# Sparse attention in a two-layer decoder: transposes of the projections held behind parts of the blocks that follow them, and other homes for the keys' rows and the compressions' sums

## The chip, the cores and the metric

The kernel runs on one core of a Trainium2 chip (trn2). A core has five engines that run side by side, each through its own queue, in order: TensorE (PE, matrix products and transposes, which write into PSUM), VectorE (DVE), ScalarE (ACT), GpSimd (POOL) and SyncE (SP, which here only issues the loads of weights from the chip's memory). The metric is the time of one execution in microseconds on the device, over several runs; lower is better.

## The reference

The input is 256 tokens of 1024 numbers. Two layers follow, each a token mixer and a squared-ReLU MLP with norms around them. The first mixer is native sparse attention, and the edit lies in it:

```python
proj = h @ w_in                       # q (16 heads x 64), then kc, vc, ks, vs, kw, vw (4 groups x 64 each), gate
q, kc_t, ks, kw = rope(q), rope(kc_t), rope(ks), rope(kw)
kcmp = silu(windows(kc_t + pos) @ w1[0]) @ w2[0]      # 15 windows of 32 tokens, 16 apart
vcmp = silu(windows(vc_t + pos) @ w1[1]) @ w2[1]
o = g0 * attend(q, kcmp, vcmp) + g1 * attend(q, selected ks, vs) + g2 * attend(q, kw, vw)
m = o @ w_out
```

With 256 tokens all four blocks of 64 are selected, so the second branch sees all causal keys. The second layer's mixer (FoX) and both MLPs are not touched.

## The kernel before, in words

Every large product is done in three: a weight and an activation are split in a high and a low part (fp32r), and `mm3` (lines 152 to 156) adds hi × hi, hi × lo and lo × hi. A weight chunk of 512 KB comes through `load_w` (line 116): SP loads it into a `raw` tile (three of them), ACT casts `hi` out of it, DVE subtracts to get `lo` (`split`, lines 112 to 114); there are six hi and six lo tiles.

The sparse mixer is a list of blocks. `c0` and `c1` are the projections kc and vc, which the compression reads; `k0`, `k1` the keys ks and kw; `v0` is vs, `v1` is vw with the gates; `q0` to `q3` are four heads of q each. Each block is 48 products on the two halves of the tokens (`nsa_block`), with two chunks of weights (v1 has three); they add up in a PSUM bank called ps_m, of which there are two. A block's evacuation (`c_evac`, `k_evac`, `q_evac`) applies rope on DVE (three operations that read the bank, and an add), and makes from it rows in SBUF (kd, kk, qs). The second step of an evacuation transposes these rows on PE into one of two ps_t banks, and ACT copies them out (tokT, kT, qT). `p0` and `p1` are the compressions (`compress`): first DVE adds positions into win (which needs tokT) and splits it, then 32 products with four chunks, whose sums ACT and DVE bring out as hs and hid; the last step transposes hid, applies silu and multiplies with w2.

The order is written in PLAN (line 45). There a name starts a block, `>p0` takes a compression one step further, `+k0` finishes an evacuation, that is, issues its transposes. S, C, V and T with numbers are the parts of the attention that follow. But this order is not the one on the engines: the framework's scheduler takes instructions as their inputs come and gives each engine a fixed list; only instructions passed to `keep_in_program_order` stand on their engine where the program has them. Before, the scheduler put a transpose among the products where it thought fit.

Of the kernel before, what the change touches and what calls it, by code (L numbers as in the profile page):

```python
# [9 lines left out]
R = mybir.dt.float32r  # L10
# [3 lines left out]
P = 128  # L14
# [6 lines left out]
G = 4  # L21
# [20 lines left out]

PLAN = "c0 +c0 v0 p0 c1 +c1 k0 k1 >p0 +k0 v1 +k1 +p0 p1 q0 >p1 +p1 | q1 q2 +q0 +q1 S02 C00 S00 S01 V00 q3 +q2 V01 S03 V02 +q3 C01 T00 S05 V03 S04 V04 S06 V05 C10 S12 S07 V06 S10 T02 S11 T01 V10 V12 V07 S15 V11 S13 C11 V13 / T03 S14 S16 T10 V16 S17 V17 V14 V15 T13 T11 T12"
SB_B = 4
FB = 2
VG = 3
# [18 lines left out]
def kernel(ctx, tc, x_in, norm_g, w_up, w_down, nsa_w_in, nsa_pos, nsa_w1, nsa_w2,  # L67
# [14 lines left out]
    def ps_tile(use):  # L82
        return psum.tile([P, 512], F32, name="ps_" + use)
# [248 lines left out]
    def c_evac(j, pv):  # L332
        kd = ev.tile([P, NT, G, 2, DH], F32, name="kd", tag="b4")
        if j == 0:
            rope(kd[:, :, :, 0, :], pv, rot)
            act.copy(kd[:, :, :, 1, :], kd[:, :, :, 0, :])
        else:
            for t in range(NT):
                v_copy(kd[:, t], pv[:, t].unsqueeze(2).broadcast_to([P, G, 2, DH]), t)
        yield  # L340
        for t in range(NT):
            pt = ps_tile("t")
            for g in range(G):
                pe.transpose(pt[:, g * P:(g + 1) * P], kd[:, t, g].rearrange("p u d -> p (u d)"), ident)
            ptv = pt.rearrange("p (g t) -> p g t", g=G)
            act.copy(tokT[j][0:DH, :, t * P:(t + 1) * P], ptv[0:DH])
            act.copy(tokT[j][DH:P, :, max(0, t * P - 1):(t + 1) * P - 1], ptv[DH:P, :, 1 - t:P])

    def k_evac(br, pk):
        kr = ev.tile([P, NT, G, DH], F32, name="kr")  # L350
        rope(kr, pk, rot)
        kks = []
        for t in range(NT):
            kk = ev.tile([P, G, 4, DH], R, name="kk", tag="b4")
            krb = kr[:, t].unsqueeze(2).broadcast_to([P, G, 2, DH])
            act.copy(kk[:, :, 0:2, :], krb)
            dve.tensor_tensor(out=kk[:, :, 2:4, :], in0=krb, in1=kk[:, :, 0:2, :].bitcast(F32), op=OP.subtract)
            kks.append(kk)
        yield
# [18 lines left out]
    def q_evac(c, pv):  # L378
# [4 lines left out]
        yield  # L383
        for t in range(NT):
            qT[t, c] = nsa1.tile([P, G, P], R, name="qT", bufs=6)
            pt = ps_tile("t")
            for j in range(G):
                pe.transpose(pt.bitcast(R)[:, j * P:(j + 1) * P], qs[:, t, j, :], ident_r)
            act.copy(qT[t, c], pt.rearrange("p (h t) -> p h t", h=G))

    def nsa_block(c0, ws=None, between=None):

        ws = ws or load_cols(W, c0, BW)
        ps = ps_tile("m").rearrange("p (t n) -> p t n", t=NT)
        hk = KD // 2 if between is None else KD
        for k0 in range(0, KD, hk):
            for t in range(NT):
                if between:

                    for i, (a, b) in enumerate(((0, 0), (0, 1), (1, 0))):  # L400
                        for k in range(KD // 2):
                            pe.matmul(ps[:, t, :], tok(hT, k, t)[a], ws[k][b], start=i + k == 0, stop=False)
                    between()
                for k in range(KD // 2 if between else k0, k0 + hk):
                    mm3(ps[:, t, :], tok(hT, k, t), ws[k], t == 0 and k == 0, t == NT - 1 and k == KD - 1)
                between = None
# [11 lines left out]
    def compress(j):  # L418
# [20 lines left out]
        hs = cp.tile([NW, CH], F32, name="hs")  # L439
        act.copy(hs, ps[64:64 + NW, 0:CH])  # L440
# [1 line left out]
        yield  # L442
        pt = ps_tile("t")
        for k in range(2):
            pe.transpose(pt[:, k * 64:k * 64 + NW], hid[:, k * P:(k + 1) * P], ident[0:NW, 0:NW])
# [6 lines left out]
        if j == 0:  # L452
            hidT = cp.tile([P, 2, P], F32, name="hidTk")
            pool.memset(hidT, 0.0)
            dve.tensor_tensor(out=hidT[:, :, 0:NW], in0=ptv, in1=sg, op=OP.mult)
            for k in range(2):
                pe.matmul(po[:, 0:P], w2[:, j, k].rearrange("p u d -> p (u d)"), hidT[:, k, :], start=(k == 0), stop=(k == 1))
            pk = po[:, 0:NW].rearrange("p (g c) -> p g c", g=G)
            split(kc[:, :, 0, 0:NC_], kc[:, :, 1, 0:NC_], pk)
        else:  # L460
            hidT = cp.tile([P, 2, G, REP, 32], F32, name="hidTv", tag="win")
            pool.memset(hidT, 0.0)
            for k in range(2):
                a, b = (v[:, k, :].rearrange("p (g c) -> p g c", g=G).unsqueeze(2).broadcast_to([P, G, REP, NC_])
                        for v in (ptv, sg))
                dve.tensor_tensor(out=hidT[:, k, :, :, 0:NC_], in0=a, in1=b, op=OP.mult)
            for g in range(G):
                for k in range(2):
                    pe.matmul(po[:, g * DH:(g + 1) * DH], hidT[:, k, g].rearrange("p r c -> p (r c)"),
                              w2[:, j, k, 0, :], start=(k == 0), stop=(k == 1))  # L470
            pv = po[:, 0:G * DH].rearrange("p (g d) -> p g d", g=G)
            for r in range(REP):
                rows = slice(r * 32, (r + 1) * 32)
                (act.copy if r % 2 else dve.tensor_copy)(vc[rows, :, r, 0:DH], pv[rows])

# [57 lines left out]
    def pair_s(t, p):  # L533
# [59 lines left out]
    env, scores, oc, on = {}, {}, {}, {}  # L593
    for cmd in PLAN.split():
        op, arg = cmd[0], cmd[1:]
        if op == "+":
            finish(env.pop(arg))
        elif op == ">":
            next(env[arg])
        elif cmd in gens:  # L600
            env[cmd] = gens[cmd]()
            if op != "v":
                next(env[cmd])
        elif op == "|":
            cmp_ctx.close()
            at = nsa_ctx.enter_context(tc.tile_pool(name="at", bufs=2))
# [441 lines left out]
```

## Time and profile before

| | |
|---|---|
| median of 3 runs | 670.02 us (667.80 to 670.09) |
| the profiled execution | 668.77 us, of which 667.0 is the span from the first to the last instruction |
| busy share of the span | PE 97%, its weight loads 85%, DVE 67%, ACT 56% |
| mean granted clock of TensorE | 0.996 of full |
| loads | 110.17 MB, 165 GB/s on the mean |

One execution was profiled, and all rows are from it, in microseconds from its first instruction. A row of a timeline gives start, length, engine, line, operation and, in brackets, how long the engine had been idle and which operation ended that. Products are pipelined, so one's length (0.28) is more than the distance to the next (0.12).

### The profile page before, as it was taken

Reading aid. Unit: us, or ns where it says so; the run is one execution under the profiler, and the core shown is the slowest. Engines: PE = TensorE matmul, PEld = TensorE weight load, DVE = VectorE, ACT = ScalarE, POOL = GpSimd, SP = SyncE. Lnnn points to the kernel's source line nnn. Section 1 sums busy time; section 2 is a strip of 40 time slices with the busy share of each in tenths; the row PEclk is TensorE's granted clock in tenths of the full one; section 3 lists DMA queues with packets and bytes.
Section 4 is the critical chain, followed back from the end, with each engine's and each line's share of the span. In section 5 each row is a group of like instructions: output and inputs, shape, how many; then the busy total and the mean of one; then the engine's idle time right before and its main releaser. Section 6 shows DMA issues by size and latency. Waiting matters only on the chain.

```text
span 667.0 us, 10515 instructions
## 1 busy us (share of the span) xinstructions
PE 649.2 (97%) x3953; PEld 564.1 (85%) x3953; DVE 445.3 (67%) x854; ACT 375.2 (56%) x654; POOL 37.6 (6%) x77
## 2 busy tenths in 40 slices
PE   7999999999999999999999999999999999999996
PEld 6999998888788888888889999987878888888884
DVE  5787898764985756556649677873967566566533
ACT  5768487765774645445537566663675445454411
POOL 1000003212100000000005000000100000000000
PEclk9998999999999999999999999999999999999999
DMA  9676853201696746656554863541667476565301
GB/s 306 179 200 192 241 168 97 64 1 60 196 305 198 230 153 217 193 164 215 166 151 115 270 216 96 158 125 35 193 185 231 149 220 190 165 213 180 104 1 63
DMA packets 74802, 110.17 MB, mean 165 GB/s; under 512 B 4696, under 2 KB 60672, under 8 KB 74752
## 3 DMA queue, kind: packets, MB, share of 16 engines
q1 hardware_dynamic: 72336, 105.48, 51.3%
q10 hardware_dynamic: 2416, 4.03, 2.0%
q8 instruction: 31, 0.51, 0.3%
q14 instruction: 19, 0.16, 0.1%
HBM read 108.44 MB, written 1.05 MB: 164 GB/s over the span
## 4 chain that ended last, share of the span: by engine, by line
PE 85%; DVE 5%; DMA 5%; ACT 2%; issue 2%; POOL 1%; SPq 0%; POOLq 0%; DVEq 0%; ACTq 0%
PE ps_m L735 14%; PE ps_m L736 8%; PE ps_m L154 6%; PE ps_m L156 6%; PE ps_m L155 6%; PE ps_o L155 5%; PE ps_s L156 5%; PE ps_s L154 5%; PE ps_o L154 5%; PE ps_s L155 5%; PE ps_o L156 5%; PE ps_o L571 3%; DVE lo L114 2%; PE ps_m L738 2%; PE ps_t L566 2%
## 5 line engine op out<-in xcount | busy, mean ns | idle before, releaser
L114 DVE TENSOR_TENSOR lo<-raw,hi 128x1024 fp32r<-128x1024 f32 (+2 forms) x196 | 237.0, 1213 | 117.4 <-ACT hi L113 110.5
L113 ACT CAST hi<-raw 128x1024 fp32r<-128x1024 f32 (+2 forms) x196 | 203.4, 1043 | 130.9 <-DMA raw<-in_mlp_w_up_dram 42.1
L735 PE MATMUL ps_m<-hT,hi 128*128 128x512 f32 x392 | 140.1, 396 | 0.0
L736 PE MATMUL ps_m<-hT,lo 128*128 128x256 f32 x448 | 116.3, 280 | 0.0
L736 PEld LDWEIGHTS ps_m<-hT,lo 128*128 128x128 f32 x448 | 84.5, 189 | 5.0
L735 PEld LDWEIGHTS ps_m<-hT,hi 128*128 128x128 f32 x392 | 73.6, 188 | 16.2
L154 PE MATMUL ps_m<-hi,hT 128*128 128x256 f32 (+3 forms) x236 | 76.3, 324 | 0.8 <-ACT hT L113 0.8
L155 PE MATMUL ps_m<-hi,hT 128*128 128x256 f32 (+3 forms) x236 | 75.6, 320 | 1.4 <-DVE hT L114 1.3
L156 PE MATMUL ps_m<-lo,hT 128*128 128x256 f32 (+3 forms) x236 | 75.2, 318 | 0.9 <-DVE lo L114 0.9
L155 PE MATMUL ps_o<-hi,ul 128*128 128x512 f32 x128 | 50.6, 396 | 0.0
L156 PE MATMUL ps_s<-lo,uh 128*128 128x512 f32 x128 | 50.6, 395 | 0.0
L154 PE MATMUL ps_o<-hi,uh 128*128 128x512 f32 x128 | 50.5, 395 | 0.0
L154 PE MATMUL ps_s<-hi,uh 128*128 128x512 f32 x128 | 50.5, 395 | 0.0
L155 PE MATMUL ps_s<-hi,ul 128*128 128x512 f32 x128 | 50.5, 394 | 0.0
L156 PE MATMUL ps_o<-lo,uh 128*128 128x512 f32 x128 | 50.4, 394 | 0.0
L154 PEld LDWEIGHTS ps_m<-hi,hT 128*128 128x128 f32 x236 | 45.2, 192 | 4.6 <-ACT hT L113 1.3
L155 PEld LDWEIGHTS ps_m<-hi,hT 128*128 128x128 f32 x236 | 45.3, 192 | 4.4 <-DVE hT L114 2.4
L156 PEld LDWEIGHTS ps_m<-lo,hT 128*128 128x128 f32 x236 | 45.1, 191 | 3.7 <-DVE lo L114 1.3
L740 ACT COPY second<-ps_m 128x256 f32<-128x256 f32 x56 | 20.8, 371 | 38.6 <-PE ps_m L738 38.6
L154 PE MATMUL ps_m<-hT,hi 128*128 128x256 f32 x128 | 37.5, 293 | 0.0
L155 PE MATMUL ps_m<-hT,lo 128*128 128x256 f32 x128 | 36.2, 283 | 0.0
L156 PE MATMUL ps_m<-hT,hi 128*128 128x256 f32 x128 | 36.1, 282 | 0.0
(242 smaller groups left out, 1107.4 us busy)
## 6 DMA issues: line engine op xcount, KB each, us to landing
raw<-in_mlp_w_up_dram SPq DMA_DIRECT2D x64, 512.0 KB, 4.1
raw<-in_mlp_w_down_dram SPq DMA_DIRECT2D x64, 512.0 KB, 4.3
raw<-in_fox_w_in_dram SPq DMA_DIRECT2D x22, 512.0 KB, 4.2
raw<-in_nsa_w_in_dram SPq DMA_DIRECT2D x18, 512.0 KB, 4.9
raw<-in_nsa_cmp_w_dram SPq DMA_DIRECT2D x8, 512.0 KB, 4.5
raw<-in_nsa_w_out_dram SPq DMA_DIRECT2D x8, 512.0 KB, 3.6
raw<-in_fox_w_out_dram SPq DMA_DIRECT2D x8, 512.0 KB, 4.3
gb<-in_norm_g_dram ACTq DMA_DIRECT2D x7, 512.0 KB, 6.6
```

Source lines behind the costliest of these rows:

```text
L113: act.copy(hi, src)
L114: dve.tensor_tensor(out=lo, in0=src, in1=hi.bitcast(F32), op=OP.subtract)
L154: queue(pe.matmul(ps, lhs[0], rhs[0], start=start, stop=False))
L155: queue(pe.matmul(ps, lhs[1], rhs[0], start=False, stop=False))
L156: queue(pe.matmul(ps, lhs[0], rhs[1], start=False, stop=stop))
L566: pe.transpose(pt[:, j * P:(j + 1) * P], sb[:, hh * 2 + br, kt * P:(kt + 1) * P], ident)
L571: pe.matmul(pov[:, hh, br, :], pts[:, j * P:(j + 1) * P], vt[:, kt, br, g, :], start=(kt == 0), stop=(kt == t))
L735: pe.matmul(psv, wh[:, fs], hT[2][:, :, k, :], start=k == 0, stop=False)
L736: pe.matmul(psv[:, 0, :], wl[:, fs], hT[0][:, k, :], start=False, stop=False)
L738: pe.matmul(psv, wh[:, fs], hT[2][:, :, k, :], start=False, stop=True)
L740: act.copy(second, psv[:, 1, :])
```

## The change

PLAN gets a name for each part of a block. A block is now a generator that the plan advances: `nsa_block` stops after each quarter (12 products), v1 after each quarter too, and the evacuations stop ahead of the transposes of each half of the tokens. The transposes, the compressions' products and the scores' products keep the place that the plan gives them. The rows kk move from a pool with two tiles (tag b4) to one with three (tag h), and the compressions' sums from a ps_m bank to a ps_s bank, which the scores use later.

```diff
-PLAN = "c0 +c0 v0 p0 c1 +c1 k0 k1 >p0 +k0 v1 +k1 +p0 p1 q0 >p1 +p1 | q1 q2 +q0 +q1 S02 C00 S00 S01 V00 q3 ...
+PLAN = ("c0 v0 v0 v0 c0 c0 v0 p0 c1 c1 c1 c1 k0 k0 k0 c1 c1 k0 k1 k1 k1 k1 p0 v1 k0 k0 v1 v1 p0 k1 k1 v1 p0 p1 "
+        "q0 q0 q0 q0 p1 q1 q1 p1 q1 q1 p1 | q2 q0 q0 q2 q1 q1 q2 q2 S02 C00 S00 S01 V00 q3 q2 q3 q2 q3 q3 V01 S03 "
...
-    def k_evac(br, pk):
+    def k_evac(br, block):
+        pk = yield from block
...
-            kk = ev.tile([P, G, 4, DH], R, name="kk", tag="b4")
+            kk = hpool.tile([P, G, 4, DH], R, name="kk", tag="h", bufs=3)
...
-        yield
         for t, kk in enumerate(kks):
+            yield
...
-                        pe.transpose(pt.bitcast(R)[:, c * P:(c + 1) * P],
-                                     kk[:, gg + g, 2 * u:2 * u + 2, :].rearrange("p u d -> p (u d)"), ident_r)
+                        tc.keep_in_program_order(pe.transpose(pt.bitcast(R)[:, c * P:(c + 1) * P],
+                                           kk[:, gg + g, 2 * u:2 * u + 2, :].rearrange("p u d -> p (u d)"), ident_r))
...
+        else:
+            for i in range(4):
+                t, k0 = i % 2, i // 2 * (KD // 2)
+                for k in range(k0, k0 + KD // 2):
+                    mm3(ps[:, t, :], tok(hT, k, t), ws[k], i == 0 and k == 0, i == 3 and k == KD - 1)
+                if i < 3:
+                    yield
...
-        ps = ps_tile("m")
+        ps = ps_tile("s")
...
-                    pe.matmul(ps[:, 0:CH], lhs, w1[u][:, i, :], start=(k + i + u == 0), stop=(k + i + u == 16))
+                    queue(pe.matmul(ps[:, 0:CH], lhs, w1[u][:, i, :], start=(k + i + u == 0), stop=(k + i + u == 16)))
...
-        if op == "+":
-            finish(env.pop(arg))
-        elif op == ">":
-            next(env[arg])
-        elif cmd in gens:
-            env[cmd] = gens[cmd]()
-            if op != "v":
-                next(env[cmd])
+        if cmd in gens:
+            if cmd not in env:
+                env[cmd] = gens[cmd]()
+            next(env[cmd], None)
```

The first place is ACT's list around c1's transposes (their copies are tokT). hi_584 to hi_626 are the four chunks of p0, hi_516 is the second of k1. Before:

```order
L113 CAST hi_516<-raw_515 128x1024
L346 COPY tokT_166<-ps_t_422 64x4x128
L347 COPY tokT_166<-ps_t_422 64x4x127
L346 COPY tokT_166<-ps_t_429 64x4x128
L347 COPY tokT_166<-ps_t_429 64x4x128
L113 CAST hi_584<-raw_583 128x1024
L113 CAST hi_598<-raw_597 128x1024
L113 CAST hi_612<-raw_611 128x1024
```

and with the change:

```order
L117 CAST hi_516<-raw_515 128x1024
L117 CAST hi_584<-raw_583 128x1024
L117 CAST hi_598<-raw_597 128x1024
L351 COPY tokT_166<-ps_t_471 64x4x128
L352 COPY tokT_166<-ps_t_471 64x4x127
L351 COPY tokT_166<-ps_t_478 64x4x128
L352 COPY tokT_166<-ps_t_478 64x4x128
L117 CAST hi_612<-raw_611 128x1024
```

The copies now stand behind the casts of two chunks of p0. On DVE win, which reads tokT, moved along: it stood ahead of the lo of p0's first chunk, and now stands behind the lo of the second and three rope operations of k0.

The second place is PE's list where p0 ends and v1 begins. ps_m_685 is v1's sum of the first half of the tokens, kk_503 and kk_506 are k0's rows. Before:

```order
L437 MATMUL ps_m_582<-lo_627,win2_352 128x256
L366 MATMUL ps_t_643<-ident_r_81,kk_503 128x128 x4
L366 MATMUL ps_t_649<-ident_r_81,kk_503 128x128 x4
L154 MATMUL ps_m_685<-hi_668,hT_115 128x304
L155 MATMUL ps_m_685<-hi_668,hT_115 128x304
L156 MATMUL ps_m_685<-lo_669,hT_115 128x304
L366 MATMUL ps_t_655<-ident_r_81,kk_506 128x128 x4
L154 MATMUL ps_m_685<-hi_668,hT_115 128x304
```

With the change twelve products of v1 stand ahead of the transposes (the last three of them, and what follows; the sum is ps_m_661 now):

```order
L158 MATMUL ps_m_661<-hi_650,hT_115 128x304
L159 MATMUL ps_m_661<-hi_650,hT_115 128x304
L160 MATMUL ps_m_661<-lo_651,hT_115 128x304
L372 MATMUL ps_t_674<-ident_r_81,kk_503 128x128 x4
L372 MATMUL ps_t_680<-ident_r_81,kk_503 128x128 x4
L158 MATMUL ps_m_661<-hi_650,hT_115 128x304
L159 MATMUL ps_m_661<-hi_650,hT_115 128x304
L160 MATMUL ps_m_661<-lo_651,hT_115 128x304
L372 MATMUL ps_t_686<-ident_r_81,kk_506 128x128 x4
```

So v1's products with its first and second chunk come ahead of k0's transposes, not behind them. On ACT the cast of p1's win, which stood behind three of the kT copies of these transposes, now stands ahead of all of them.

The third place is ACT's list where p1's sums come out (hs_918). hi_957 is the second chunk of q1, hi_1021 and hi_1027 are those of q2. Before:

```order
L113 CAST qs_857<-qr_851 128x8x64
L113 CAST hi_957<-raw_956 128x1024
L440 COPY hs_918<-ps_m_860 60x256
L113 CAST hi_1021<-raw_1020 128x1024
L448 ACTIVATE sg_924<-ps_t_921 128x120
```

and with the change, where hi_928 is the second chunk of q1:

```order
L117 CAST hi_928<-raw_927 128x1024
L117 CAST qs_857<-qr_851 128x8x64
L117 CAST hi_1021<-raw_1020 128x1024
L456 COPY hs_918<-ps_s_860 60x256
L117 CAST hi_1027<-raw_1026 128x1024
```

The copy now stands behind one chunk more, and on DVE hid stands behind that chunk's lo in the same way. On PE the transposes of hid stood behind 15 products of q1 and now stand behind 24. The lists of SP and POOL are the same before and after.

## Rows read from the trace of the kernel before

**Rows 1.** The head of the page.

```profile
span 667.0 us, 10515 instructions
```

**Rows 2.** Table by stretch: busy time of each engine, clock, share of DMA, GB/s.

```profile
20.00:44.00 24.00, 24.00 (x202) 23.85 (x201) 18.81 (x20) 17.02 (x24) 0.00 (x0) 1.00 0.73 202
48.00:56.00 8.00, 6.32 (x40) 5.76 (x38) 6.48 (x10) 7.24 (x13) 0.96 (x1) 0.79 0.74 211
72.00:75.00 3.00, 2.10 (x18) 1.84 (x17) 1.95 (x4) 2.42 (x3) 0.00 (x0) 1.00 0.65 193
88.00:110.00 22.00, 20.55 (x164) 19.10 (x164) 19.43 (x87) 18.77 (x46) 3.77 (x8) 1.00 0.43 142
110.00:160.00 50.00, 49.89 (x364) 44.95 (x363) 30.45 (x150) 32.44 (x73) 11.69 (x24) 1.00 0.11 33
```

**Rows 3.** The same table, finer, around 50 us; the clock is third from last.

```profile
51.00:52.00 1.00, 0.78 (x5) 0.79 (x6) 1.00 (x3) 1.00 (x3) 0.00 (x0) 0.50 0.81 255
...
54.00:56.00 2.00, 2.00 (x15) 2.00 (x14) 1.49 (x2) 1.97 (x3) 0.96 (x1) 0.91 1.00 317
```

**Rows 4.** Timeline of PE: c1's, k0's and hid's transposes, v1's first lo.

```profile
32.41 0.66 PE L344 MATMUL ps_t<-ident,kd 128*128 128x128 f32 x4
...
47.87 0.80 PE L366 MATMUL ps_t<-ident_r,kk 128*128 128x128 f32 x8
...
49.53 0.41 PE L156 MATMUL ps_m<-lo,hT 128*128 128x304 f32 x1 [0.40 <-DVE lo L114]
51.22 0.75 PE L366 MATMUL ps_t<-ident_r,kk 128*128 128x128 f32 x4 [1.28 <-ACT kT L368]
...
74.68 0.33 PE L445 MATMUL ps_t<-ident,hid 60*128 60x60 f32 x2 [0.90 <-DVE hid L441]
```

**Rows 5.** SP's queue until 100 us: waits, landing, the load of p0.2.

```profile
SPq L127 <- DVE lo L114: 49.1, 22, 6.3
...
DMA to landing us min/median/max: 3.5/4.4/8.4
...
32.60 0.37 SPq L127 DMA_DIRECT2D raw<-in_nsa_cmp_w_dram  x1
```

**Rows 6.** Timeline of ACT: tokT, hi of p0.2, of v1, hs, win, q2.1.

```profile
34.02 0.57 ACT L346 COPY tokT<-ps_t 64x512 f32<-64x512 f32 x1
...
39.23 1.05 ACT L113 CAST hi<-raw 128x1024 fp32r<-128x1024 f32 x1 [1.79 <-DMA raw<-in_nsa_cmp_w_dram]
...
48.39 1.75 ACT L113 CAST hi<-raw 128x912 fp32r<-128x912 f32 x2 [1.56 <-PE ps_t L366]
50.04 0.36 ACT L440 COPY hs<-ps_m 60x256 f32<-60x256 f32 x1
...
52.68 1.01 ACT L113 CAST win<-win 128x960 fp32r<-128x960 f32 x1
...
73.07 0.37 ACT L440 COPY hs<-ps_m 60x256 f32<-60x256 f32 x1
73.40 1.05 ACT L113 CAST hi<-raw 128x1024 fp32r<-128x1024 f32 x1
```

**Rows 7.** Timeline of DVE: win, lo of p0.2, p0.3, p0.4, v1.1, hid, q2.1.

```profile
36.41 1.88 DVE L426 TENSOR_TENSOR win<-tokT,posT 128x960 f32<-128x960 f32 x1 [1.04 <-ACT tokT L347]
...
40.31 1.23 DVE L114 TENSOR_TENSOR lo<-raw,hi 128x1024 fp32r<-128x1024 f32 x1 [0.91 <-ACT hi L113]
...
42.72 1.22 DVE L114 TENSOR_TENSOR lo<-raw,hi 128x1024 fp32r<-128x1024 f32 x1
...
44.76 1.23 DVE L114 TENSOR_TENSOR lo<-raw,hi 128x1024 fp32r<-128x1024 f32 x1 [0.22 <-ACT hi L113]
...
48.37 1.10 DVE L114 TENSOR_TENSOR lo<-raw,hi 128x912 fp32r<-128x912 f32 x1
...
74.22 0.41 DVE L441 TENSOR_TENSOR hid<-ps_m,hs 60x256 f32<-60x256 f32 x1
74.55 1.21 DVE L114 TENSOR_TENSOR lo<-raw,hi 128x1024 fp32r<-128x1024 f32 x1
```

More of the change, by code (lines that the diff above doesn't have):

```diff
@@ L41 @@
 E0 = 1
-PLAN = "c0 +c0 v0 p0 c1 +c1 k0 k1 >p0 +k0 v1 +k1 +p0 p1 q0 >p1 +p1 | q1 q2 +q0 +q1 S02 C00 S00 S01 V00 q3 +q2 V01 S03 V02 +q3 C01 T00 S05 V03 S04 V04 S06 V05 C10 S12 S07 V06 S10 T02 S11 T01 V10 V12 V07 S15 V11 S13 C11 V13 / T03 S14 S16 T10 V16 S17 V17 V14 V15 T13 T11 T12"
+PLAN = ("c0 v0 v0 v0 c0 c0 v0 p0 c1 c1 c1 c1 k0 k0 k0 c1 c1 k0 k1 k1 k1 k1 p0 v1 k0 k0 v1 v1 p0 k1 k1 v1 p0 p1 "
[3 rows of a table added]
 SB_B = 4
@@ L330, with c_evac @@
     dve.tensor_copy(posT.rearrange("p j l -> p (j l)"), ps[:, 0:32])
-    def c_evac(j, pv):
+    def c_evac(j, block):
+        pv = yield from block
         kd = ev.tile([P, NT, G, 2, DH], F32, name="kd", tag="b4")
@@ L339, in c_evac @@
                 v_copy(kd[:, t], pv[:, t].unsqueeze(2).broadcast_to([P, G, 2, DH]), t)
-        yield
         for t in range(NT):
+            yield
             pt = ps_tile("t")
             for g in range(G):
-                pe.transpose(pt[:, g * P:(g + 1) * P], kd[:, t, g].rearrange("p u d -> p (u d)"), ident)
+                tc.keep_in_program_order(pe.transpose(pt[:, g * P:(g + 1) * P], kd[:, t, g].rearrange("p u d -> p (u d)"), ident))
             ptv = pt.rearrange("p (g t) -> p g t", g=G)
@@ L358, in k_evac @@
             kks.append(kk)
-        yield
         for t, kk in enumerate(kks):
+            yield
             for gg in range(0, G, 2):
@@ L376, in gate_evac, with q_evac @@
             dve.tensor_scalar(out=gt[t][:, :, 0], in0=gt[t][:, :, 0], scalar1=rowv[:, 0:1], scalar2=None, op0=OP.mult)
-    def q_evac(c, pv):
+    def q_evac(c, block):
+        pv = yield from block
         qr = ev.tile([P, NT, G, DH], F32, name="qr", tag="kr")
@@ L382, in q_evac @@
         split(qs[..., 0:DH], qs[..., DH:P], qr)
-        yield
         for t in range(NT):
+            yield
             qT[t, c] = nsa1.tile([P, G, P], R, name="qT", bufs=6)
@@ L387, in q_evac @@
             for j in range(G):
-                pe.transpose(pt.bitcast(R)[:, j * P:(j + 1) * P], qs[:, t, j, :], ident_r)
+                tc.keep_in_program_order(pe.transpose(pt.bitcast(R)[:, j * P:(j + 1) * P], qs[:, t, j, :], ident_r))
             act.copy(qT[t, c], pt.rearrange("p (h t) -> p h t", h=G))
@@ L394, in nsa_block @@
         ps = ps_tile("m").rearrange("p (t n) -> p t n", t=NT)
-        hk = KD // 2 if between is None else KD
-        for k0 in range(0, KD, hk):
+        if between:
             for t in range(NT):
+                k1 = 0
                 if between:
+                    k1 = KD // 2
                     for i, (a, b) in enumerate(((0, 0), (0, 1), (1, 0))):
-                        for k in range(KD // 2):
+                        for k in range(k1):
                             pe.matmul(ps[:, t, :], tok(hT, k, t)[a], ws[k][b], start=i + k == 0, stop=False)
                     between()
-                for k in range(KD // 2 if between else k0, k0 + hk):
+                for k in range(k1, KD):
                     mm3(ps[:, t, :], tok(hT, k, t), ws[k], t == 0 and k == 0, t == NT - 1 and k == KD - 1)
                 between = None
+        else:
[4 more added lines that the diff above has]
+                if i < 3:
+                    yield
         return ps.rearrange("p t (g d) -> p t g d", g=G)
@@ L444, in compress @@
         for k in range(2):
-            pe.transpose(pt[:, k * 64:k * 64 + NW], hid[:, k * P:(k + 1) * P], ident[0:NW, 0:NW])
+            tc.keep_in_program_order(pe.transpose(pt[:, k * 64:k * 64 + NW], hid[:, k * P:(k + 1) * P], ident[0:NW, 0:NW]))
         ptv = pt[:, 0:128].rearrange("p (k n) -> p k n", k=2)[:, :, 0:NW]
@@ L455, in compress @@
             dve.tensor_tensor(out=hidT[:, :, 0:NW], in0=ptv, in1=sg, op=OP.mult)
+            yield
             for k in range(2):
-                pe.matmul(po[:, 0:P], w2[:, j, k].rearrange("p u d -> p (u d)"), hidT[:, k, :], start=(k == 0), stop=(k == 1))
+                queue(pe.matmul(po[:, 0:P], w2[:, j, k].rearrange("p u d -> p (u d)"), hidT[:, k, :], start=(k == 0),
+                                stop=(k == 1)))
             pk = po[:, 0:NW].rearrange("p (g c) -> p g c", g=G)
@@ L466, in compress @@
                 dve.tensor_tensor(out=hidT[:, k, :, :, 0:NC_], in0=a, in1=b, op=OP.mult)
+            yield
             for g in range(G):
                 for k in range(2):
-                    pe.matmul(po[:, g * DH:(g + 1) * DH], hidT[:, k, g].rearrange("p r c -> p (r c)"),
-                              w2[:, j, k, 0, :], start=(k == 0), stop=(k == 1))
+                    queue(pe.matmul(po[:, g * DH:(g + 1) * DH], hidT[:, k, g].rearrange("p r c -> p (r c)"),
+                                    w2[:, j, k, 0, :], start=(k == 0), stop=(k == 1)))
             pv = po[:, 0:G * DH].rearrange("p (g d) -> p g d", g=G)
@@ L476, in v_block @@
     def v_block():
-        pv = nsa_block(1792)
+        pv = yield from nsa_block(1792)
         for t in range(NT):
@@ L485, in vg_block @@
             ps = ps_tile("m")
-            proj_nat(ps[:, 0:nvw], hT, t, ws)
+            for k in range(KD):
+                mm3(ps[:, 0:nvw], tok(hT, k, t), ws[k], k == 0, k == KD - 1)
+                if k == KD // 2 - 1:
+                    yield
             v_copy(vt[:, t, 1, :, 0:DH], ps[:, 0:BW].rearrange("p (g d) -> p g d", g=G), t)
             gate_evac(t, ps[:, BW:nvw])
+            if t == 0:
+                yield
     at = at_ctx = None
@@ L546, in pair_s @@
             for u in range(2):
-                pe.matmul(o, qT[t, h // 4][:, h % 4, :], kT[:, :, g, u, 0:nk], start=(u == 0), stop=(u == 1))
+                queue(pe.matmul(o, qT[t, h // 4][:, h % 4, :], kT[:, :, g, u, 0:nk], start=(u == 0), stop=(u == 1)))
         for i in range(4):
```

2 rows, old and new, of the table PLAN are left out of this document.

## The prediction

> **What bounds the kernel now.** I read the page first: a span of 667.0 us [rows 1]. The profiled execution took 668.77 us, 1.77 around its span; the median of the three timed runs is 670.02, 1.25 above it, and they spread over 2.3 us. The sum below is made against 668.77 and carried to the median by adding the change alone. 0.5% is 3.35 us, about what a measurement of this kernel can tell from no change.
>
> The table by stretch comes next [rows 2]. The edited code runs from 20 to about 100 us. From 20 to 44 TensorE (PE) is busy all the time, 202 products in 24 us, so 0.12 us from one 256-column product to the next. It idles 1.68 us between 48 and 56, with a mean granted clock of 0.79 there, 0.90 us between 72 and 75, and 1.45 us between 88 and 110; from 110 to 160 it is busy 49.89 of 50. What the edited stretch gains or loses therefore reaches the end nearly whole, and the most that it can give back is what PE loses there.
>
> The PE timeline says who ended those waits [rows 4]. At 49.53 the first product of v1 that reads a lo tile waited 0.40 for VectorE (DVE); at 51.22 the transposes of k0's rows waited 1.28 for ScalarE (ACT) to copy kT out of one of the two ps_t banks; at 74.68 the transpose of hid waited 0.90 for DVE. The clock followed the second: it was granted at half (0.50, 1.2 GHz instead of 2.4) from 51 on, and 0.91 over 54 to 56 puts its return at 54.4 [rows 3]. Of these 3.4 us, 3.2 had products in them, which is 1.6 us lost. After the 0.90 at 74 it stayed full [rows 2]. So the edit could win back at most 0.40 + 1.28 + 1.6 + 0.90 = 4.2 us, plus some of the 1.45 after 88.
>
> Behind the waits stands one loop. The kernel has three raw tiles, so a weight chunk is asked for when DVE finishes the lo of the chunk three before; it lands 4.4 us later (median), ACT makes hi in 1.05 and DVE lo in 1.23 [rows 5 to 7]. SP's waits for lo are its longest, 49.1 us by 100 us [rows 5]. That is 6.7 us for three chunks even with no queue, and each of these chunks feeds PE for 0.96 us (p0, p1) to 2.9 us (a projection). I number the chunks by block: p0.1 to p0.4, v1.1 to v1.3, q0.1, q0.2, p1.1 to p1.4, q1.1, q1.2, q2.1.
>
> **The change, part by part.** No instruction that computes is added or removed, and SP's and POOL's orders are unchanged; what moves is the order on PE, ACT and DVE.
>
> *c1's transposes* went after 7 products of k0, at 32.41 [rows 4], so k0 began about 31.5; now 36 products stand ahead, so 31.5 + 4.3 = 35.8. On PE this costs nothing, they are the same eight. On ACT the four tokT copies, 2.4 us in all from 34.02, now stand behind the hi of p0.1 and p0.2, and the latter waited for its DMA until 39.23 [rows 6]. On DVE win (1.88 us, at 36.41) needs them and now stands behind k0's first three rope operations instead of ahead of p0.1's lo [rows 7]. p0.2 was asked for at 32.60 [rows 5] and landed only 6.6 us later; with the median of 4.4 it lands at 37.1, hi ends at 38.2, the copies end at 40.6. DVE then runs lo of p0.2 from 38.25, rope (40.31 to 42.72 holds lo and rope, so 2.4 in all), win from 40.65, the fourth rope operation, lo of p0.3 from 43.05. From there to v1.1's lo it took 5.65 us (42.72 to 48.37) [rows 7], now less the rope operation (0.6, between 42.72 + 1.22 and 44.76, less the 0.22 of idleness there) and that 0.22: v1.1's lo starts at 47.9 and ends at 49.0, against 49.47.
>
> *v1 and the transposes of k0's rows.* PE leaves p0 at 47.87 as before (p0.3's lo ends at 44.3, needed at 46.1). Now v1's products come first: two, then a wait for lo until 49.0 (0.85); nine more to 50.3; the twelfth needs v1.2's lo, which follows v1.1's on DVE and ends at 50.8 (0.5). Eight transposes and three products bring PE to 52.1. The next transposes need ps_t back. ACT's queue ahead of that copy: hi of v1.2 (to 49.65), hi of v1.3, hs, kk, two fills of win, the 1.0 us cast of win, then kT, so 53.2; before, the cast of win stood behind three kT copies [rows 6]. PE waits 1.15, and 0.2 at the next pair. The waits add to 2.7 us where before they were 0.40 + 1.28 + 1.6 by the clock = 3.3. If the clock holds, PE gains 0.6; if it falls as it did, it loses 1.0. Next, k1's transposes have six products between them and one kT copy, which stands behind the hi of p1.1: 0.4 more. PE leaves p1 at 71.6 or, with the half clock, 73.2; before 71.8 (the wait before 74.68 began at 73.8, after 15 products of q1 and the last one's tail).
>
> *p1's sums, q1 and hid.* This decides. The hs copy and hid's sum stood behind q1.2 on both engines: hs at 73.07, hid at 74.22 [rows 6, 7]. Now they stand behind q2.1, the next chunk: its hi ran from 73.40, its lo from 74.55 to 75.76. Is q2.1 earlier? It closes the loop p0.4, v1.3, p1.1, p1.4, q2.1. By the orders above p0.4's lo ends 0.6 earlier (45.4 against 45.99), but v1.3's now has a kk of k1 ahead of it on DVE besides hid; between 44.76 + 1.23 and 48.37 lie two such kk and three rope operations of 1.2 in all, so a kk is 0.6 [rows 7]. The two even out; I take q2.1's lo as before, 75.76, with 1 us either way for what the later links add. hid then ends at 76.1 and its transposes go at 76.2, against 74.68: 1.52 later. But 24 products of q1 now stand ahead of them, not 15, so 9 × 0.12 = 1.08 us of work is done by then. The difference is 0.44 us lost. As PE is there by 74.5 (or 76.1 with the half clock), this wait swallows what v1 gained or lost.
>
> *q1's to q2's transposes and the first scores:* the same products in another order, with rope and qs hidden behind 23 and 13 products of q2. PE's waits here were 1.45 us in 22; nothing in the rows prices the new order, so 0, between -1.45 (all of them gone) and +1.0 (one more wait like that for hid).
>
> *Homes.* ps_s for p0's and p1's sums costs nothing, the banks stand idle until the scores. No PE wait named a ps_m bank [rows 4], so it gains nothing either. A third tile for kk would let ACT cast k1's rows sooner, but that cast stands behind hs and its rope on DVE, so 0. By the Trainium skill (Perfetto Trace Analysis, Matmuls) groups should rotate through different PSUM banks so that an evacuation overlaps the next group; it would make v1 start freely, which the trace shows it already did but for lo.
>
> **Sum:** 668.77 + 0.44 = 669.2, on the median's scale 670.02 + 0.44 = **670.4 us**; with the bounds of the last three parts (1 either way for q2.1, -1.45 and +1.0 for the scores) 668.0 to 672.9.
>
> **The rivals.**
>
> *Faster.* The waits of v1 and hid go and the clock stays full: 670.0 - 4.2 = 665.8. It needs q2.1's hi to be done when p1 ends at 71.7 (it started at 73.40), and kT's copy not to wait behind win's cast. For it: PE's transposes are spread and 24 products stand ahead of hid. Against: the chunk loop, which the edit doesn't shorten. 0.24.
>
> *A clock that falls at q1.* The wait for hid is now 76.2 - 74.5 = 1.7 us; 1.28 (with 0.40 before it) lowered the clock at 51, 0.90 at 74 did not. Price 1.6 us: 672.0, still within 0.5%. 0.13.
>
> *Slower: tokT behind p0.2's chunk.* If p0.2 lands as late as it did (39.2), hi ends at 40.3, the copies at 42.7, win runs from there, and v1.1's lo ends at 51.1. PE then waits 2.9 us at 48.15, and p0.4's lo is 1.6 late, which the loop hands down to hid: 77.8 instead of 76.2. Alone that is 670.4 + 1.6 = 672.0; with PE idle over 3 us at q1 the clock falls too, 673.7. It decides from about 1.5 us of delay on that chunk. ACT idle for 1.79 us ahead of that hi [rows 6] speaks for it, the median landing against. 0.16. The Trainium skill (TensorE: Matmul & The Clock Gate, Part 1, on engine queue depths) says that ACT's and DVE's queues are strict FIFO. The trace agrees: hs at 50.04 stood behind two casts that began at 48.39, though p0's sum had ended by 48.1 [rows 4, 6]. Were it otherwise, tokT would go at 36.3 and this rival would fall.
>
> *The forecast,* no difference that can be told, has 0.47. So faster 0.24, same 0.47 + 0.13 = 0.60, slower 0.16. The range, 665.5 to 673.5, reaches to both outer rivals and leaves out about half of each; the likeliest case alone is 668.0 to 672.9.
>
> **What would show it.** Right: in the profile after, win runs on DVE after k0's rope; v1's third product waits for lo near 49, kk's later transposes for ACT's kT; the transposes of hid wait over 1.2 us at about 76, released by DVE; q2 ends where it did, near 88. Wrong: if hid's transposes go without a wait, or before 75.2, the loop was shorter than I made it, and the time falls by 1 us or more; if the first lo of v1 ends after 50.5, the third rival has happened. If the time moves by over 3 us and the stretch from 20 to 100 us doesn't show it, the cause lies in the scores, which I put at nothing.

## The result, and the profile after

The changed kernel took 673.27 us, median of 13 runs (670.12 to 676.19), against 668.43 for the kernel before beside it (13 runs, 666.62 to 670.25): ratio 1.0074, 95% interval 1.0060 to 1.0089. By the ratio it is slower by 4.95 us (the medians differ by 4.84). Its profiled execution took 672.53 us, 2.13 around a span of 670.4.

The head of the page after, and the table by stretch with the columns of [rows 2]:

```profile
span 670.4 us, 10503 instructions
```

```profile
20.00:44.00 24.00, 24.00 (x204) 24.00 (x203) 17.80 (x19) 17.45 (x24) 0.00 (x0) 1.00 0.70 203
48.00:56.00 8.00, 5.23 (x32) 4.92 (x31) 8.00 (x13) 5.67 (x12) 0.31 (x1) 0.79 0.65 191
72.00:75.00 3.00, 3.00 (x28) 3.00 (x27) 1.73 (x3) 1.76 (x3) 0.00 (x0) 1.00 0.75 222
75.00:88.00 13.00, 11.07 (x84) 10.80 (x83) 10.09 (x16) 7.43 (x11) 0.56 (x2) 0.87 0.63 184
88.00:110.00 22.00, 20.87 (x178) 20.12 (x176) 19.95 (x78) 17.24 (x38) 3.41 (x7) 1.00 0.45 147
110.00:160.00 50.00, 49.64 (x344) 44.60 (x345) 32.67 (x159) 34.28 (x79) 11.22 (x24) 0.97 0.13 42
```

Between 48 and 56 PE now idles 2.77 us (1.68 before), while DVE is busy all 8 us of it: the engine that makes lo is late and has no slack. Between 75 and 88, all busy at full clock before, PE idles 1.93 and the clock is 0.87. The row of before for that stretch:

```profile
75.00:88.00 13.00, 13.00 (x112) 12.88 (x112) 11.83 (x18) 7.64 (x12) 0.56 (x2) 1.00 0.73 207
```

The same table after, finer, shows three places at half clock, where [rows 3] had one (a fourth, from 11.1 to 14.5, lies ahead of all edits):

```profile
52.00:55.00 3.00, 3.00 (x18) 2.97 (x17) 3.00 (x5) 2.51 (x6) 0.00 (x0) 0.50 0.79 198
79.00:82.00 3.00, 3.00 (x18) 3.00 (x17) 2.97 (x6) 1.27 (x2) 0.00 (x0) 0.55 0.88 235
110.00:113.00 3.00, 2.69 (x10) 2.51 (x11) 2.65 (x14) 2.75 (x10) 0.35 (x2) 0.51 0.41 158
```

PE's timeline, for [rows 4]:

```profile
36.26 1.04 PE L349 MATMUL ps_t<-ident,kd 128*128 128x128 f32 x8
...
51.37 0.41 PE L160 MATMUL ps_m<-lo,hT 128*128 128x304 f32 x1 [2.77 <-DVE lo L118]
...
77.66 0.33 PE L461 MATMUL ps_t<-ident,hid 60*128 60x60 f32 x2 [1.93 <-DVE hid L457]
```

SP's, for [rows 5], the load of p0.2:

```profile
33.29 0.37 SPq L131 DMA_DIRECT2D raw<-in_nsa_cmp_w_dram  x1
```

ACT's, for [rows 6]: hi of p0.2, the first tokT copy, hi of p0.3, hi of q2.1, hs.

```profile
38.94 1.05 ACT L117 CAST hi<-raw 128x1024 fp32r<-128x1024 f32 x1 [0.43 <-DMA raw<-in_nsa_cmp_w_dram]
39.89 0.58 ACT L351 COPY tokT<-ps_t 64x512 f32<-64x512 f32 x1
...
42.27 1.05 ACT L117 CAST hi<-raw 128x1024 fp32r<-128x1024 f32 x1
...
74.71 1.05 ACT L117 CAST hi<-raw 128x1024 fp32r<-128x1024 f32 x1
75.78 0.37 ACT L456 COPY hs<-ps_s 60x256 f32<-60x256 f32 x1
```

DVE's, for [rows 7]: lo of p0.2, win, lo of p0.3 and p0.4, the low part of the rows kk, lo of v1.1, of q2.1, hid.

```profile
40.02 1.23 DVE L118 TENSOR_TENSOR lo<-raw,hi 128x1024 fp32r<-128x1024 f32 x1 [0.26 <-ACT hi L117]
...
42.43 1.86 DVE L442 TENSOR_TENSOR win<-tokT,posT 128x960 f32<-128x960 f32 x1
...
44.82 2.34 DVE L118 TENSOR_TENSOR lo<-raw,hi 128x1024 fp32r<-128x1024 f32 x2
47.74 1.29 DVE L363 TENSOR_TENSOR kk<-kr,kk 128x512 fp32r<-128x512 f32 x2 [0.58 <-ACT kk L362]
...
50.21 1.10 DVE L118 TENSOR_TENSOR lo<-raw,hi 128x912 fp32r<-128x912 f32 x1
...
76.06 1.22 DVE L118 TENSOR_TENSOR lo<-raw,hi 128x1024 fp32r<-128x1024 f32 x1
77.20 0.41 DVE L457 TENSOR_TENSOR hid<-ps_s,hs 60x256 f32<-60x256 f32 x1
```

The reader follows one delay through three engines. c1's transposes ended at 37.3, but their copies stood on ACT behind hi of p0.2, which waited for its chunk until 38.94; win ran at 42.43 instead of 36.41; the lo of p0.3 began at 44.82 instead of 42.72, that of v1.1 at 50.21 instead of 48.37; and at the end of the loop of chunks hid came at 77.20 instead of 74.22. Of each of these differences 0.7 us was there ahead of all edits: c0's transposes came at 23.87 in this execution, at 23.17 before.

Where the time of this execution went can be summed between places that have the same work ahead of them on PE's list. From q1's first product to the last transposes of q3 it took 35.31 us (72.69 to 108.00), before 33.00 (71.83 to 104.83). That is 2.31 more: 1.03 for the longer wait for hid, 0.28 for other waits and 1.7 for the half clock behind hid, less 0.7 that the same products and transposes took in their new order. From there to the last transposes of the attention's result it took 57.63, before 56.66: 0.97, and the half clock from 110 lies in it. From c0's transposes to q1 it is 0.16 more: the 1.2 us more of waiting and half clock at v1 are nearly made up by PE's new order, in which the same work took 0.41 less already up to p0, without a wait in either. With the 0.70 us ahead of the edits that makes 4.14 us at the last transposes of the attention's result; the rest of the execution took 0.76 less than before, so the spans differ by 3.4.

### The profile page after: what moved, and what is told of

The parts are those of the page before. It is cut to its first block, busy times and chain, and to the rows that moved or that the text cites. A ratio compares the mean times of both kernels' runs of the same rounds, so it can differ in the third digit from the quotient of the medians.

```text
span 670.4 us, 10503 instructions
## 1 busy us (share of the span) xinstructions
PE 650.1 (97%) x3953; PEld 566.8 (85%) x3953; DVE 445.4 (66%) x854; ACT 375.6 (56%) x654; POOL 37.6 (6%) x77
## 4 chain that ended last, share of the span: by engine, by line
PE 83%; DVE 6%; DMA 5%; ACT 3%; issue 2%; POOL 1%; SPq 0%; POOLq 0%; DVEq 0%; ACTq 0%
PE ps_m L755 14%; PE ps_m L756 8%; PE ps_m L158 6%; PE ps_m L160 6%; PE ps_m L159 5%; PE ps_o L158 5%; PE ps_o L159 5%; PE ps_o L160 5%; PE ps_s L160 5%; PE ps_s L158 5%; PE ps_s L159 5%; PE ps_o L595 3%; DVE lo L118 3%; DMA raw<-in_nsa_w_in_dram 3%; PE ps_m L758 2%; PE ps_s L571 2%
## 5 line engine op out<-in xcount | busy, mean ns | idle before, releaser
L160 PE MATMUL ps_m<-lo,hT 128*128 128x256 f32 (+3 forms) x236 | 76.2, 323 | 3.2 <-DVE lo L118 3.2
L159 PE MATMUL ps_m<-hi,hT 128*128 128x256 f32 (+3 forms) x236 | 76.4, 324 | 1.4 <-DVE hT L118 1.3
L158 PE MATMUL ps_m<-hi,hT 128*128 128x256 f32 (+3 forms) x236 | 77.1, 327 | 0.3 <-ACT hT L117 0.3
L159 PEld LDWEIGHTS ps_m<-hi,hT 128*128 128x128 f32 x236 | 46.3, 196 | 4.3 <-DVE hT L118 2.4
L158 PEld LDWEIGHTS ps_m<-hi,hT 128*128 128x128 f32 x236 | 46.2, 196 | 3.8 <-ACT hT L117 0.6
```

Source lines behind the costliest of these rows:

```text
L158: queue(pe.matmul(ps, lhs[0], rhs[0], start=start, stop=False))
L159: queue(pe.matmul(ps, lhs[1], rhs[0], start=False, stop=False))
L160: queue(pe.matmul(ps, lhs[0], rhs[1], start=False, stop=stop))
```

## The experiments

Each was timed against runs of the kernel before on its own chip; the medians of before differ by up to 2.7 us between chips, so ratios are compared, not times. Diffs are against the changed kernel's PLAN unless said.

**1 to 4: the two waits one at a time, and the homes.**

```diff
 e1
-c1 c1 c1 c1 k0 k0 k0 c1 c1 k0
+c1 c1 c1 c1 k0 c1 c1 k0 k0 k0
 e2
-p1 q1 q1 p1 q1 q1 p1 | q2 q0 q0 q2
+p1 q1 q1 q1 q1 p1 q2 q0 q0 p1 | q2
 e3: e1 and e2 together
 e4, on the kernel before
-            kk = ev.tile([P, G, 4, DH], R, name="kk", tag="b4")
+            kk = hpool.tile([P, G, 4, DH], R, name="kk", tag="h", bufs=3)
-        ps = ps_tile("m")
+        ps = ps_tile("s")
```

> The change with one thing undone: c1's transposes stand behind 12 products of k0 instead of 36. DVE's list then has win ahead of the lo of p0.1 again, as before the change. Theory A (the copies of tokT behind the casts of p0's chunks hold win up, win holds up the lo of p0.3 to v1.1, and the chunk loop hands that down to hid): v1's first lo ends before 50.2 and PE waits under 1.5 us for it instead of 2.77, hid's transposes go before 76.9 instead of 77.66, and the time falls by 1.6 to 4 us, to a ratio of 1.001 to 1.005 against the kernel before. Theory B (the cost is made at q1, where hs and hid stand behind q2.1): v1's wait falls, but hid's transposes still go at 77.2 or later and the time falls by less than 1 us (ratio over 1.0055). Theory C (the cost lies in q2's to q3's transposes and the first scores, 88 to 110 us): the waits before 80 may go, the stretch from 88 to 110 stays as it is, and the ratio stays over 1.0055.

Measured: 1.0031 (1.0016 to 1.0046), 2.9 us less than the change, with intervals that don't overlap; 0.4 of it lies outside the span (2.2 us around it in the change, 1.8 here). DVE's and PE's timelines of it (win, lo of v1.1; v1's first lo, hid) and the clock in four stretches:

```profile
37.19 1.87 DVE L442 TENSOR_TENSOR win<-tokT,posT 128x960 f32<-128x960 f32 x1 [1.04 <-ACT tokT L352]
...
48.88 1.10 DVE L118 TENSOR_TENSOR lo<-raw,hi 128x912 fp32r<-128x912 f32 x1
```

```profile
50.04 0.41 PE L160 MATMUL ps_m<-lo,hT 128*128 128x304 f32 x1 [1.25 <-DVE lo L118]
```

```profile
76.63 0.33 PE L461 MATMUL ps_t<-ident,hid 60*128 60x60 f32 x2 [2.35 <-DVE hid L457]
```

```profile
52.00:55.00 3.00, 2.94 (x27) 2.60 (x26) 2.90 (x5) 2.98 (x6) 0.64 (x1) 1.00 0.96 283
78.00:81.00 3.00, 3.00 (x16) 3.00 (x16) 2.69 (x5) 1.23 (x2) 0.00 (x0) 0.50 0.96 299
109.00:112.00 3.00, 2.67 (x10) 2.48 (x11) 2.64 (x14) 2.76 (x10) 0.39 (x2) 0.50 0.40 160
112.00:115.00 3.00, 3.00 (x11) 2.40 (x11) 1.43 (x7) 1.17 (x3) 0.00 (x0) 0.50 0.62 175
```

Theory A, in each of its numbers: v1's wait is 1.25 and the clock stays up there. But PE, now earlier at q1, waits longer for hid, and the half clock behind that stays. Near 110 the half clock of this execution (108.4 to 115.3) is longer than the change's (110.0 to 113.5).

> The change with one thing moved: the transposes of p1's hid stand behind all of q1 (48 products) instead of half of it, and p1's last products behind q2's first 12 and q0's transposes. Theory A (lateness begins at win): the wait for hid (1.93 us) goes, but it was only where the lateness came out; q2's products need q2.1's lo, which is as late as before, so PE waits about as long there, and the time falls by under 1.5 us. Theory B (the place of hid is the cost): PE runs on through q1, no wait over 0.5 us between 74 and 82 and no half clock there, and the time falls by 1.9 us of waiting and 1.6 of half clock, 3.5 us, to a ratio near 1.002. Theory C (cost after 88): no change of 1 us.

Measured: 1.0055 (1.0037 to 1.0074). No wait for hid, no half clock at 79, yet little comes back, because PE stands a few products later at q0's transposes:

```profile
83.17 0.54 PE L395 MATMUL ps_t<-ident_r,qs 128*128 128x128 f32 x4 [2.08 <-ACT qT L396]
```

The clock stayed full behind this wait:

```profile
83.00:86.00 3.00, 2.83 (x23) 2.67 (x23) 3.00 (x5) 2.19 (x5) 0.00 (x0) 1.00 0.40 160
```

Theory B's 3.5 us did not come; A's under 1.5 did (1.3), though the interval overlaps the change's.

> Both moves together: c1's transposes behind 12 products of k0, and hid's behind all of q1. Theory A: as with the first move alone, within 1 us. Theory B: as with the second alone, within 1 us. If each makes a part of its own, the two falls add up and the ratio is 0.998 to 1.002. Theory C: still over 1.0055.

Measured: 1.0041 (1.0024 to 1.0057), the first run's within 1 us, as A has it.

> The kernel before with the other homes alone: the compressions' sums in a ps_s bank, and keys' rows in the pool with three tiles; PLAN and the order of the transposes as before. The prediction puts this at nothing: a ratio within 0.998 to 1.002. A rival: a third tile for keys' rows lets casts of k1's rows in ahead of casts that feed PE, and some of the loss of the change is made here: a ratio over 1.003.

Measured: 1.0006 (0.9988 to 1.0024): no difference that can be told, as predicted.

**5 to 8: k0's transposes, the part behind the bar, the clock.**

```diff
 e5
-p0 v1 k0 k0 v1 v1 p0
+p0 k0 k0 v1 v1 v1 p0
 e6: e1 and e5 together
 e7
-| q2 q0 q0 q2 q1 q1 q2 q2 S02 C00 S00 S01 V00 q3 q2 q3 q2 q3 q3 V01
+| q2 q2 q2 q2 q0 q0 q1 q1 S02 C00 S00 S01 V00 q3 q3 q3 q3 q2 q2 V01
 e8: e1, and ahead of hid's transposes (mm3's three products are also written out in v1)
+        if j == 1:
+            idle_products(9)
```

> The change with another thing undone: the 16 transposes of k0's rows stand ahead of v1's products again, not behind the first 12; c1's stay behind 36 products of k0. In the order that follows, hs and hid also move: they stand ahead of q2.1's casts, directly behind q1.2's. Theory A (lateness made by win and handed down by the chunks): v1's first lo still ends near 51.3, the 16 transposes fill 1 to 2 us of that wait, but q2.1 is as late as before, so what hid no longer waits q2 waits; the ratio stays over 1.005. Theory B (hid's place behind q2.1 costs on its own): hid's transposes go before 76.3 with a wait under 0.7 us and no half clock at 79; 1.9 us of waiting and up to 1.7 us of clock come back, a ratio of 1.002 to 1.005.

Measured: 1.0087 (1.0066 to 1.0109). v1's first lo still waits, and hid's transposes go without a wait, but hardly earlier:

```profile
50.89 0.41 PE L160 MATMUL ps_m<-lo,hT 128*128 128x304 f32 x1 [1.74 <-DVE lo L118]
...
77.27 0.33 PE L461 MATMUL ps_t<-ident,hid 60*128 60x60 f32 x2
```

So a wait at hid that is gone gave nothing back while the chunks are late: B falls. What that wait costs alone this run can't say, since its profile has longer stretches of half clock than the change's (51.3 to 58.1 and 109.3 to 116.1) and another order of the second half of the attention (see e6).

> Both undone: c1's transposes behind 12 products of k0, the transposes of k0's rows ahead of v1; hs and hid ahead of q2.1's casts. If what the first run left over (a ratio of 1.0031) is the wait for hid (2.35 us there) and the half clock behind it, both go: v1's first lo ends before 50.2, hid's transposes go before 75.5 with a wait under 1 us, and the ratio is 0.998 to 1.002. If it is made after 88 us (order of q2's and q3's transposes, a clock that falls near 108), these waits go and the ratio stays over 1.003.

Measured: 1.0050 (1.0030 to 1.0069). The wait for hid went (its transposes at 75.70, 0.2 later than expected, and no half clock at q1), and the time didn't: the second branch. Other waits came in its place, 0.57 us for v1's lo, 1.39 for kT behind it and 1.24 for q1's chunks. Two rows by stretch show another part of the loss, 107 to 113 at half clock:

```profile
107.00:110.00 3.00, 2.29 (x11) 1.92 (x9) 1.87 (x16) 2.60 (x9) 0.80 (x2) 0.50 0.56 178
110.00:113.00 3.00, 2.90 (x9) 2.51 (x10) 1.62 (x5) 2.33 (x6) 0.31 (x1) 0.50 0.28 61
```

A further part may be an order that none of my edits names. With TensorE's work ahead of it moved, the scheduler placed the free instructions of the attention's second half otherwise: e2, e3 and e7 have one other list, e5 and e6 a second, e8 a third; the change, e1 and e4 have the list of before there.

> The change with only its last part undone: behind the bar in PLAN the order is that of before (q2 whole, then q0's and q1's transposes; q3 whole, then q2's). Theory C (cost made after 80 us by the transposes of q0 to q2 among the products, and by the clock that falls near 108 us): the time falls by 1.5 us or more, to a ratio of 1.005 or less. Theories A and B: the waits for v1's lo (2.8 us) and for hid (1.9 us) stay and the ratio stays at 1.0074, within 0.0015.

Measured: 1.0050 (1.0032 to 1.0068), 1.6 us less than the change, though the intervals overlap, with waits for v1's lo (2.4) and hid (2.1) near the change's. C may hold for a part. The half clock at 110 is gone from this profile, but another order is there, and its price can be read without a clock that falls. From the first to the last transposes of the attention's result, in the kernel before and in this one:

```profile
108.41 0.38 PE L582 MATMUL ps_t<-ident,on 128*128 128x128 f32 x2
...
161.49 0.33 PE L582 MATMUL ps_t<-ident,on 128*128 128x128 f32 x1 [0.15 <-POOL on L576]
```

```profile
111.74 0.38 PE L606 MATMUL ps_t<-ident,on 128*128 128x128 f32 x2
...
165.84 0.33 PE L606 MATMUL ps_t<-ident,on 128*128 128x128 f32 x1 [0.17 <-POOL on L600]
```

53.08 and 54.10 us for the same instructions at full clock: 1.0 us, of which 0.4 is waits, none over 0.31. That is one profile of each; the list of e8 took 53.29, also at full clock.

> The kernel of the first run (c1's transposes early), with nine products of zeros, which nothing reads, ahead of the transposes of p1's hid: 9 x 0.21 us fill 1.9 us of the 2.35 us in which PE waits there. They compute nothing of the result. If the half clock that follows that wait (from 77.7) is a cost of its own, it is gone, q1 and q2 run at full clock, and the ratio falls from 1.0031 by 1.7 us, to about 1.0005. If the half clock costs nothing, because q2 then waits for its chunks or the scores for theirs, the waits after 80 us grow by as much and the ratio stays within 0.001 of 1.0031.

Measured: 1.0120 (1.0095 to 1.0146), a miss. The products filled the wait (18 passes of 2.17 us in all) and the half clock at q1 was gone, but the scheduler, counting them as work, set the steps of hidTv behind q3's chunks (first row; the second is v1's wait for its lo, which was 1.25 in the first run):

```profile
PE ps_o L490 <- DVE hidTv L486: 2.5, 1, 2.5
PE ps_m L513 <- DVE lo L118: 2.1, 1, 2.1
```

The clock's price at q1 is not settled by this run.

**9 to 12: put back in groups.**

```diff
 e9
-k0 k0 k0 c1 c1 k0 k1 k1 k1 k1 p0 v1 k0 k0 v1 v1 p0 k1 k1 v1 p0 p1 q0 q0 q0 q0 p1 q1 q1 p1 q1 q1 p1 |
+k0 c1 c1 k0 k0 k0 k1 k1 k1 k1 p0 k0 k0 v1 v1 v1 v1 k1 k1 p0 p0 p1 q0 q0 q0 q0 p1 q1 p1 q1 q1 p1 q1 |
 e10: e9 and e7 together
 e11, from e9
-p1 q1 p1 q1 q1 p1 q1 |
+p1 q1 q1 p1 q1 q1 p1 |
 e12: e1 and e7 together
```

> Everything that the change moves ahead of the bar in PLAN is put back as near to before as its parts allow: c1's transposes behind 12 products of k0, k0's ahead of v1 and k1's behind it, p0's last steps behind v1, p1's hid transposed behind 15 products of q1. Behind the bar the change stands (q0's and q1's transposes inside q2, q2's inside q3); from the last transposes of q3 on TensorE's list is that of before word for word. Theory: the cost is made ahead of the bar, and by the order of the second half of the attention that the scheduler then chooses; so here the waits of 44 to 75 us are those of before within 0.5 us, TensorE reaches the last transposes of q3 within 0.6 us of before (measured from c1's first rows, kd), and the ratio is 0.998 to 1.0025. Rival: the transposes inside q2 and q3 cost by themselves (they did in the run that undid only them: 1.6 us): q3's last transposes come 1 us or more later than before, ratio over 1.003.

Measured: 1.0033 (1.0018 to 1.0049). Its waits between 20 and 115 us are each those of before within 0.3, and q3's last transposes come 2.0 us earlier after kd (c0's rows; the expectation miscalls them), about 1.6 of it because the half clock that the profile of before has at 51 is not in this one:

```profile
PE ps_t L372 <- ACT kT L374: 1.3, 2, 1.1
PE ps_t L461 <- DVE hid L457: 0.9, 1, 0.9
PE ps_s L571 <- DVE mx L574: 0.6, 1, 0.6
PE ps_m L160 <- DVE lo L118: 0.6, 1, 0.6
```

The ratio is the rival's, though its interval reaches into the theory's range, and the rival's sign in the profile, q3's transposes later by 1 us or more, did not come. That what stands behind the bar costs by itself is therefore not shown. The profile is of one of the run's faster executions (span 666.4, mean 667.1), and on another chip than the profile of before.

> The same, with the part behind the bar put back too: TensorE's list from q1 on is that of before, so what is left of the change is the homes, transposes kept in the plan's order, and a few products more ahead of c1's and k0's transposes. All theories: a ratio of 0.998 to 1.002. If it is over 1.003, the cost lies in none of the moves tried, but in holding the order by hand or in the homes.

Measured: 1.0013 (0.9999 to 1.0026), as all had it. It is 0.0020 or 1.3 us under the ninth run, which would be the price of the part behind the bar, but the intervals overlap; the twelve times of each, from one chip, differ by 1.0 us on the mean, give or take 1.1. The profiles don't show such a price either: from q1's first product to q3's last transposes the ninth run took 32.56 us (70.13 to 102.70), the tenth 32.75 (70.99 to 103.74). The mean clock over its runs is 0.9951, that of the ninth 0.9934.

> The first of these with hid's transposes behind 24 products of q1, as the change has them (hs and hid ahead of q2.1's casts, as in before). The scheduler then gives the second half of the attention another order (transposes of the probabilities and the products with v stand otherwise among the products of w_out), the same as in the second, third and sixth run. If that order costs, as those traces suggest (54.1 us or more from the first to the last transposes of the attention's result, 53.1 before, with no half clock in one of them), the ratio is 0.0015 or more above that of the first of these; if it does not, the two agree within 0.001.

Measured: 1.0048 (1.0032 to 1.0064), 0.0015 above the ninth: as expected, but the intervals overlap, and 0.3 us of it lies outside the span (2.1 around it, 1.8 in the ninth). Between the two transposes of the attention's result its profile has 54.7 us, the ninth's 54.0, both with about 2 us of half clock at the start. Its list there is that of the fifth and sixth runs; the second and third have another, so the expectation is wrong in that.

> The two moves that gained most, together: c1's transposes behind 12 products of k0 (alone 1.0031 against 1.0074 for the whole change, so 0.0043), and the part behind the bar as in before (alone 1.0050, so 0.0024). Everything else is the change's: k0's transposes inside v1, hid's behind 24 products of q1, the homes. If the two are losses of their own, they add: 1.0074 - 0.0043 - 0.0024 = 1.0007, or 1.000 to 1.002. If both gave back the same loss (lateness that comes out as half clock near 110 us, whichever of them is taken away), the ratio is 1.0025 or more.

Measured: 1.0050 (1.0031 to 1.0069). The two don't add: with the part behind the bar put back, the first run's kernel came out 1.3 us slower, not faster, though the intervals overlap. But it isn't the rival's half clock near 110 either: in its profile the clock is full there, and between 20 and 115 us it is halved only behind the wait for hid:

```profile
76.00:78.00 2.00, 2.00 (x11) 2.00 (x11) 1.97 (x3) 0.62 (x2) 0.00 (x0) 0.50 0.80 249
110.00:113.00 3.00, 2.99 (x22) 2.46 (x20) 2.68 (x11) 2.58 (x5) 0.00 (x0) 1.00 0.50 175
```

It has the order of the seventh run (54.45 us between the two transposes), hid's wait of 1.9 again, and 1.6 for v1's lo, whose chunk p0.2 took longer to land than in any other profile (6.9 us).

No version beat the kernel before; the fourth and the tenth can't be told from it.

## Why the prediction came out as it did

The forecast was no difference; what came has the mechanism of the slower rival, "tokT behind p0.2's chunk", which had 0.16. That 673.27 us lies within the range of 665.5 to 673.5 is luck: the kernel before measured 668.43 beside it, 1.59 less than the 670.02 that the range was built on, and the ratio of 1.0074 on 670.02 is 675.0.

**The step that failed** is the landing of p0.2's chunk. I took the queue's median of 4.4 us and kept the row's 6.6 for the rival. In the 14 profiles of this study that chunk took 5.2 to 6.9 us, never near the median; here 5.6. So hi ended at 40.0 (38.2 in the forecast), the copies at 42.2 (40.6; rival 42.7), v1.1's lo at 51.3 (49.0; rival 51.1), PE waited 2.77 (0.85; rival 2.9), and hid's transposes went at 77.66 (76.2; rival 77.8). Of the 2.3 us at v1.1's lo, 1.2 are the landing, 0.7 the later start of this execution (the chunk was asked for at 33.29, not 32.60), and most of the rest is a wait of 0.58 that DVE has at 47.74 for ACT's kk, which the forecast did not have. So without the later start v1.1's lo and hid come between the forecast and the rival, not at the rival; the landing alone was under the 1.5 us of delay at which the prediction put the turn. The first run shows the cause: with the copies ahead of that cast again, 2.9 us of the 4.95 come back. The Trainium skill (TensorE: Matmul & The Clock Gate, Part 1, on engine queue depths) states that ACT's queue is strict FIFO; the trace agrees, since the copies stood from 37.3 to 39.9 with their inputs done, 0.43 us of it with ACT idle.

**v1.** Its waits for kT (1.15 and 0.2) were not seen, since PE came later. They were not seen either in the first run, where v1's lo came 1.3 us earlier and k0's transposes stand as in the change. The half clock was.

**hid.** That q2.1's cast and lo stand ahead of hs and hid was right, and the wait is DVE's. The rival has PE idle over 3 us there; it idled 1.93, and the clock fell all the same. The first run is near the likeliest case with the clock of the rival "a clock that falls at q1": hid at 76.63, half clock behind it, 2.0 us by the prediction, 0.0031 or 2.1 us measured (1.1 to 3.1). Its profile has a longer half clock near 110 too, for which the prediction has no term, so the agreement may be chance. Taking the wait for hid away gave little (1.3 us in the second run, where it moved to q0's transposes) or nothing (fifth).

**q1's to q2's transposes** were put at nothing, between -1.45 and +1.0. The runs don't settle it: undone in the change they gave 1.6 us, undone in the ninth run 1.3, undone in the first run they lost 1.3, each time with overlapping intervals. From q1's first product to q3's last transposes the change took 35.31 us and the seventh run 35.66. So no profile shows the moved transposes themselves to cost.

**Homes:** no difference that can be told, as put.

**The sum.** The rival has 0.44 + 1.6 + 1.6 = 3.64 us, measured were 0.0074 x 668.4 = 4.95 (4.0 to 5.9 by its interval). In the two profiles the parts are other ones: 0.16 + 2.31 = 2.47 up to q3's transposes, where the rival's terms lie, 0.97 behind them and 0.36 outside the span, to which the rival gives nothing. The two executions differ by 3.76; the rest up to the medians' 4.84 is that the change's was 0.74 faster than its median and that of before 0.34 slower. So the 0.0043 that the first run gave back is shown to come from the place of c1's transposes, and how the other 2.1 us divide stays open. Two sums of the prediction are off: the upper bound of the likeliest case is 670.4 + 1 + 1.0 = 672.4, not 672.9, and by its own steps the rival's win is 2.05 us later than the forecast's (42.7 against 40.65), not the 1.6 that it hands down to hid.

## What to carry to other kernels

Before a copy is moved behind a cast that waits for a load, take that load's own landing, not its queue's median, and follow what needs the copy: here it was a DVE operation ahead of the next four chunks. A wait that ends a loop of loads is where lateness comes out, not where it is made; taking it away moved it to the next consumer. When times of two profiles are set side by side, take off what one execution was already late ahead of the edit. Where a scheduler fills the rest, two moves that seem to gain apart need not add: compare the free part's order too.

## What the runs showed of the chip

In the change the granted clock fell to half three times behind PE's waits: at 52 after 2.77 us, at 79 after 1.93, and at 110 after 0.8 and 0.6 close together. The length of one wait does not tell it here: after 2.08 us at 83 in the second run the clock stayed full. Whether it fell near 110 differed from run to run: of the change's 13 runs the eight with a mean clock of 0.991 or more have a median of 672.45 us, the five at 0.987 or less 674.94, and the profiles of the fourth and tenth runs, whose times can't be told from those of before, have half clock from 107.3 and 106.9. So a half clock there in one profile is not by itself a cost of the change. The time around the span was 1.8 us in the kernel before and five of the twelve, 1.9 in one, and 2.0 to 2.2 in the change and six others; nothing in the traces says why.
